# Gate and up products of 18 of 22 FFN tiles as seven block products for eight

## The chip, the cores and the metric

The kernel runs on one core of one Trainium2 chip. The metric is the device time of one execution, in microseconds (us). Of the kernel before, three runs took 2164.84 to 2165.06 us, median 2164.97.

## What is computed

Two layers of a streaming encoder trunk over 576 tokens: a sample stream of 64 and a prompt of 512. Each layer has three attention branches and then a gated feed-forward network (FFN), which is the part that the change touches:

```
xn = x * rsqrt(mean(x*x) + EPS) * g            # RMSNorm, D_MODEL 1024
gu = xn @ w_up                                 # 1024 x (2 * 2816): gate half, up half
c  = conv_b + sum over kk of conv_w[kk] * (gate with its two rows of state ahead)[t + kk]
x += (gelu(c) * up) @ w_down                   # 2816 x 1024
```

Inputs and outputs are float32.

## The kernel before

The tokens lie along the free dimension, features on the partitions, so the residual stream x is eight tiles `x1_00` to `x1_07` of 128x576. A TensorE product covers 288 tokens (a "half": the first has the 64 sample tokens and 224 of the prompt, the second 288 of the prompt). Every float32 product is made of two fp32r parts: each weight and each token tile is split into a high part (a cast by ScalarE) and a low part (source minus high, by VectorE), and three matmuls of 128x128 by 128x288 (hi·hi, hi·lo, lo·hi) are summed in PSUM (`mm`, L131 in the trace).

The 2816 columns of the FFN are 22 tiles f. Per tile there are two chunks: gate `g` (8 blocks of the 1024 rows x 2 halves x 3 = 48 matmuls into PSUM tiles `mg`) and up `u` (48, into `mu`). `ffn_f` (L1236) writes what follows them: VectorE multiplies the gate's product by the norm factor `R` into the convolution's input `gp`; ScalarE and VectorE make the convolution `c` (one activation, two scalar_tensor_tensor of 578 columns); ScalarE makes the gelu `ge`; VectorE makes `ur` = up x R; GpSimd multiplies `ge` by `ur`; ScalarE and VectorE split the result into `hh` and `hl`. The down product runs by groups of tiles, `FG = [2, 4, 4, 4, 4, 4]`: `down` (L1312) makes four chunks `d2` per group, each with two column blocks x two halves, every one of those four blocks a sum over the tiles of the group (3 matmuls per tile: 12 in a group of four, 6 in the group of two). Its PSUM tiles `md` come from a pool of two banks (`pmm`), and VectorE adds each block to x (`x<-md,x`). The four down chunks of a group follow one another after the first tile of the next group.

The order of the work is written by hand. `chunk` lists the chunks; `run_main` (L424) goes through them, emits the matmuls and, between them (`tick`), lets generators (`gens`) emit a step each, by a clock `clk` that adds up assumed costs per engine. `fetch` (L375, loads at L383) is called two chunks ahead and issues the load of a raw weight tile (128x8x128, 512 KB) on SyncE's queue; `split` (L385) makes its high and low parts one chunk ahead. So each engine runs a fixed list in order, and an instruction that waits holds what is behind it on its engine. All operations of ScalarE, VectorE and GpSimd go through one helper, and have the line L102 in the trace.

Of the kernel before, what the change touches and what calls it, by code (L numbers as in the profile page):

```python
# [16 lines left out]
P = 128  # L17
# [24 lines left out]
FG = [2, 4, 4, 4, 4, 4]  # L42


@with_exitstack
def trunk_kernel(ctx: ExitStack, tc: tile.TileContext, a: dict, o: dict):
# [16 lines left out]
    def slot(nm, dt=F32):  # L63
        return sp_.tile([P, TOK], dt, tag="s", name=nm, bufs=NS)

    def wide(tag, nm, dt=F32):
        return ap_.tile([P, 1280], dt, tag=tag, name=nm, bufs=2)
# [80 lines left out]
    def tick():  # L148
        now = clk["PE"]
        went = False  # L150
        for it in list(gens):
            if it[2] <= now and (it[0] == "w" or max(clk["ACT"], clk["DVE"]) < now + LAG):
                step(it)
                went = True
# [121 lines left out]
    def load_tables():  # L276
# [7 lines left out]
        t5t = sm.tile([32, 4], F32, tag="t5", name="t5t", bufs=1)  # L284
# [36 lines left out]
    def setup(aid, tabs, t5t, oh):  # L321
# [11 lines left out]
        for l in range(DEPTH):  # L333
# [5 lines left out]
            lt = sm.tile([P, 64], F32, tag="lt", name=f"lt{l}", bufs=1)  # L339
# [28 lines left out]
    def chunk(nm, src, kt, act, evac, ncol=1, pre=None, pre_ev=None, post=None, norm=None, half=None, twin=None):  # L368

        chunks.append(dict(nm=nm, src=src, kt=kt, act=act, evac=evac, ncol=ncol, pre=pre, pre_ev=pre_ev, post=post,  # L370
                           norm=norm, half=half))
# [3 lines left out]
    def fetch(i):  # L375
# [3 lines left out]
        if c["src"] is None:  # L379
            return  # L380
# [43 lines left out]
    def run_main(start):  # L424
        for i in range(start, len(chunks)):
# [3 lines left out]
            drain("w")  # L429
            fetch(i + 2)  # L430
            if i + 1 < len(chunks):
                spawn("w", split(i + 1), True)
            kt = c["kt"]
# [129 lines left out]
    def load_bias_sample(rows, nm):  # L563
        b = ap_.tile([P, 192], F32, tag="bias_s", name=f"biass{nm}", bufs=1)
# [5 lines left out]
    def natural(u, src, off, kind):  # L570
# [8 lines left out]
        nat = sm.tile([P, 4, P], F32, tag="nat", name=f"nat{kind}{nm}", bufs=1)  # L579
# [9 lines left out]
        else:  # L589
            nats = sm.tile([T, P], F32, tag="natsk", name=f"natsk{nm}", bufs=1)  # L590
# [8 lines left out]
    def prep_v(u):  # L599
# [6 lines left out]
        VS = ap_.tile([P, 4, 2, P], F32R, tag="VS", name=f"VS{nm}", bufs=2)  # L606
# [12 lines left out]
    def prep_k(u):  # L619
# [3 lines left out]
        KD = ap_.tile([P, 2, S], F32R, tag="KD", name=f"KD{nm}", bufs=1)  # L623
# [22 lines left out]
    def prep_q(u):  # L646
# [4 lines left out]
        X = ap_.tile([P, 2, S], F32R, tag="X", name=f"X{nm}", bufs=1)  # L651
# [133 lines left out]
    def sample_soft(u, nm, b):  # L785
# [6 lines left out]
        A = sm.tile([P, 256], F32, tag="sa", name=f"sA{nm}", bufs=1)  # L792
# [55 lines left out]
    def sample_b(u):  # L848
# [10 lines left out]
        A = sm.tile([P, 256], F32, tag="sa", name=f"sA{nm}", bufs=1)  # L859
# [11 lines left out]
    def head_b(u, e):  # L871
# [5 lines left out]
        ch = ap_.tile([P, 512], F32R, tag="bias", name=f"ch{nm}", bufs=2)[:, 0:384]  # L877
# [840 lines left out]
```

## Time and profile before

| | |
|---|---|
| median of 3 runs | 2164.97 us (2164.84 to 2165.06) |
| profiled execution, its own time | 2164.78 us |
| its span in the profile | 2163.0 us |
| mean granted TensorE clock | 0.999 of full |
| TensorE busy | 2135.8 us, 99% of the span, 15911 matmuls and transposes |
| VectorE, ScalarE, GpSimd busy | 64%, 48%, 18% |
| moved by DMA | 200.5 MB, mean 93 GB/s |

The FFN of layer 0 runs from about 659 to 1080 us, that of layer 1 from about 1722 to 2140 us. Matmuls are pipelined: the duration printed for one is longer than the distance to the next, so the rate is read from the distances of starts, or from a run of many in the chain of waits. A step on VectorE likewise can start a little ahead of the printed end of the one before.

### The profile page before, as it was taken

What the parts mean: (1) busy time and instruction counts of PE and PEld (TensorE: products, weight loads), DVE (VectorE), ACT (ScalarE), POOL (GpSimd) and SP (SyncE); (2) the same over time, 40 slices, a digit from 0 to 9 for tenths busy, and PEclk for the clock granted to TensorE, in tenths of its full rate; (3) what the DMA queues carried; (4) which work ended last, traced back from release to release, by engine and by line L of the source; (5) the groups of instructions that cost most, each with busy time, mean ns of one, the idle gap of its engine ahead of it and who ended that gap; (6) DMA issues with size and microseconds to landing.
All of it is one profiled execution on the core that took longest, in us unless ns stands there. A gap on an engine that the chain in (4) does not pass through costs nothing.

```text
span 2163.0 us, 39766 instructions
## 1 busy us (share of the span) xinstructions
PE 2135.8 (99%) x15911; PEld 2099.8 (97%) x15911; DVE 1393.0 (64%) x2860; ACT 1041.3 (48%) x2057; POOL 398.1 (18%) x523
## 2 busy tenths in 40 slices
PE   8999999999999999999999999999999999999998
PEld 7999999999999999999999999999999999999998
DVE  7886667767466655556678765667765566555564
ACT  5657776555434322323355677755554333222334
POOL 2111121111122111212110122201102112111221
PEclk9999999999999999999999999999999999999999
DMA  7442222223332322222243222233323322222222
GB/s 216 122 139 84 73 85 80 89 79 97 93 118 60 101 84 82 85 79 88 88 139 107 83 73 73 73 93 98 99 74 122 88 79 81 86 78 88 78 89 65
DMA packets 326563, 200.50 MB, mean 93 GB/s; under 512 B 10544, under 2 KB 320754, under 8 KB 326314
## 3 DMA queue, kind: packets, MB, share of 16 engines
q1 hardware_dynamic: 324618, 194.88, 30.6%
q0 software_dynamic: 1760, 3.08, 0.4%
q8 instruction: 125, 2.05, 0.4%
q14 instruction: 60, 0.49, 0.1%
HBM read 176.54 MB, written 25.83 MB: 94 GB/s over the span
## 4 chain that ended last, share of the span: by engine, by line
PE 92%; DVE 5%; issue 1%; ACT 1%; POOL 1%; DMA 0%; SPq 0%; DVEq 0%; POOLq 0%; ACTq 0%
PE md L131 11%; PE mg1f L131 6%; PE mg0f L131 6%; PE mu0f L131 6%; PE mu1f L131 6%; PE mo L131 4%; PE mg0a L131 2%; PE mg1a L131 2%; PE mg0b L131 2%; PE mg1b L131 2%; PE mg0c L131 2%; PE mg1c L131 2%; DVE wlod L102 1%; PE mb1a L131 1%; PE mb0a L131 1%
## 5 line engine op out<-in xcount | busy, mean ns | idle before, releaser
L102 DVE TENSOR_TENSOR x<-md,x 128x288 f32<-128x288 f32 x192 | 86.9, 455 | 117.2 <-PE md L131 116.3
L102 ACT CAST whid<-wrd 128x512 fp32r<-128x512 f32 (+1 forms) x88 | 46.8, 579 | 138.1 <-PE md L131 87.9
L131 PE MATMUL md<-hh0f,whid 128*128 128x288 f32 x352 | 104.9, 298 | 3.5 <-DVE x L102 3.5
L131 PE MATMUL mu0f<-xhf,wlou0f 128*128 128x288 f32 x352 | 103.8, 295 | 0.0
L131 PE MATMUL mu1f<-xhf,wlou1f 128*128 128x288 f32 x352 | 103.8, 295 | 0.0
L131 PE MATMUL md<-hh0f,wlod 128*128 128x288 f32 x352 | 103.8, 295 | 0.0
L131 PE MATMUL mg1f<-xhf,whig1f 128*128 128x288 f32 x352 | 103.7, 295 | 0.0
L131 PE MATMUL mg0f<-xhf,whig0f 128*128 128x288 f32 x352 | 103.7, 295 | 0.0
L131 PE MATMUL mg0f<-xhf,wlog0f 128*128 128x288 f32 x352 | 103.7, 295 | 0.0
L131 PE MATMUL mg1f<-xhf,wlog1f 128*128 128x288 f32 x352 | 103.7, 295 | 0.0
L131 PE MATMUL mu1f<-xlf,whiu1f 128*128 128x288 f32 x352 | 103.7, 295 | 0.0
L131 PE MATMUL mu0f<-xlf,whiu0f 128*128 128x288 f32 x352 | 103.7, 295 | 0.0
L131 PE MATMUL mu0f<-xhf,whiu0f 128*128 128x288 f32 x352 | 103.6, 294 | 0.0
L131 PE MATMUL mu1f<-xhf,whiu1f 128*128 128x288 f32 x352 | 103.6, 294 | 0.0
L131 PE MATMUL md<-hl0f,whid 128*128 128x288 f32 x352 | 103.6, 294 | 0.0
L131 PE MATMUL mg0f<-xlf,whig0f 128*128 128x288 f32 x352 | 103.6, 294 | 0.0
L131 PE MATMUL mg1f<-xlf,whig1f 128*128 128x288 f32 x352 | 103.6, 294 | 0.0
L131 PE MATMUL md<-hh1f,whid 128*128 128x288 f32 x288 | 85.7, 297 | 2.7 <-DVE x L102 2.7
L131 PE MATMUL md<-hh1f,wlod 128*128 128x288 f32 x288 | 84.9, 295 | 0.0
L131 PE MATMUL md<-hl1f,whid 128*128 128x288 f32 x288 | 84.8, 294 | 0.0
L131 PE MATMUL mo<-ml,whio 128*128 128x288 f32 x256 | 75.6, 295 | 0.8 <-DVE ml L102 0.8
L131 PE MATMUL mo<-mh,wloo 128*128 128x288 f32 x256 | 75.5, 295 | 0.0
(960 smaller groups left out, 8434.1 us busy)
## 6 DMA issues: line engine op xcount, KB each, us to landing
wrd<-in_w_down SPq DMA_DIRECT2D x40, 512.0 KB
wrg0f<-in_w_up SPq DMA_DIRECT2D x22, 512.0 KB
wru0f<-in_w_up SPq DMA_DIRECT2D x22, 512.0 KB
wrg1f<-in_w_up SPq DMA_DIRECT2D x22, 512.0 KB
wru1f<-in_w_up SPq DMA_DIRECT2D x22, 512.0 KB
wro<-in_w_out SPq DMA_DIRECT2D x16, 512.0 KB
xspill<-x SPq DMA_DIRECT2D x16, 288.0 KB
x<-xspill SPq DMA_DIRECT2D x16, 288.0 KB
```

The costliest lines, as they stand in the source:

```text
L102: return f(*args, **kw)
L131: nc.tensor.matmul(out, lhsT=lhsT, rhs=rhs, start=start, stop=stop, skip_group_check=True)
```

## The change

With the token halves h0 and h1, the rows of the weights cut into a top and a bottom half of 512, and gate and up as the two output blocks, gate and up of one tile are a product of 2x2 blocks: A11, A12 (gate, top and bottom rows), A21, A22 (up) times y11, y12 (top rows of y = x·g·R, halves h0, h1), y21, y22 (bottom rows). Eight block products of 12 matmuls each make 96. From tile NORD = 4 on, the change uses a seven-product scheme of Strassen's kind (84 matmuls), in the order A11, P, R, A12, Q, A22, V, with P = A21 + A22, R = A21 + A11, Q = P + A11, V = Q + A12.

- **Token side.** Once per layer, `forms` (L1320) makes y and its differences on VectorE in slots `ya`, `yb`, `tp`, `tq`, and their high and low parts `fh`, `fl` for seven forms, beside tiles 0 to 3. Some lows are a subtraction on VectorE, others (`low`, L1346) a copy of minus the high part by ScalarE and then an accumulating DMA of the source, issued on GpSimd's queue.
- **Weight side.** Per tile, `wforms` (L1386) loads A11|A12 (raw tile `wr..0`), A22 (`wr..3`) and A21 twice (`wr..1`), 1.25 MB for 1 MB. Two accumulating DMAs add A22 and A11 to the two copies of A21, which gives P and R. Two additions on VectorE give Q and V (`wr..2`). The high parts are casts by ScalarE; the lows of A11 and A12 (`wlo..a`) and of A22 (`el..d0`) are by ScalarE and accumulating DMA, those of P and R (`el..b0`, `el..b1`) and of Q and V (`wlo..c`) by VectorE.
- **Results.** `unit_f` (L1438) emits the 84 matmuls (A12 adds into the bank of A11, Q into that of P) and the combining: three kinds of copies by ScalarE (`s`, `gp`), five operations of VectorE (`z`, `u`, `s`, `u`, `gp`). No multiplication by R is left there, and the product ge·u moves from GpSimd to VectorE (`tail`, L1521).
- **Down product.** A down chunk follows each tile (two of them follow tiles 4 and 5, which belong to the first group of two tiles), with loads and splits of its own in slots (`down_own`, L1416: `dr` raw, `dh`, `dl`), where before four chunks ran in a row.
- **Memory.** The tiles of attention, FFN and end live in pools by phase; `gp`, `c`, `ge` move into slots.

```diff
...
 FG = [2, 4, 4, 4, 4, 4]
+NORD = 4
+GW = TOK + 4
...
+    phase = {"p": tc.alloc_tile_pool(name="att0", bufs=1, reuse_waits="tile")}
+    def next_phase(nm):
+        phase["p"].release()
+        phase["p"] = tc.alloc_tile_pool(name=nm, bufs=1, reuse_waits="tile")
+    def ptile(shape, dt, tag, name, bufs):
+        return phase["p"].tile(shape, dt, tag=tag, name=name, bufs=bufs)
     def wide(tag, nm, dt=F32):
-        return ap_.tile([P, 1280], dt, tag=tag, name=nm, bufs=2)
+        return ptile([P, 1280], dt, tag=tag, name=nm, bufs=2)
...
+            if c["own"] and c["src"] is None:
+                c["act"]()
+                continue
+            if c["own"]:
+                drain_while(lambda: not c.get("hi"), c["nm"])
...
+            chunk(f"u{nm}", a["w_up"][l][:, F + f * P:F + (f + 1) * P], ND, act, evu, pre_ev=pre_u, post=post_u,
+                  pre=(lambda: spawn("wf", wforms(NORD))) if f == NORD - 1 else None)
...
+        def forms():
+            R = cur["R"]
+            two = lambda t: t.rearrange("p (b c) -> p b c", b=2)
+            for k in range(4):
+                y1, y2, t12, t34 = (two(slot(f"{n}{l}{k}")) for n in ("ya", "yb", "tp", "tq"))
+                for y, d in ((y1, k), (y2, k + 4)):
+                    vector.scalar_tensor_tensor(y.rearrange("p b c -> p (b c)"), in0=x[d], scalar=gffn(l, d),
+                                                in1=R, op0=ALU.mult, op1=ALU.mult)
+                    yield
...
+                fh, fl = fast["fh"][k], fast["fl"][k]
+                for j, n, src in ((0, 1, y1[:, 0:1, :]), (1, 2, y2), (3, 2, t12), (5, 2, t34)):
+                    hi = fh[:, j:j + n, :]
+                    scalar.copy(hi, src)
+                    yield
+                    low(fl[:, j:j + n, :], src, hi, n == 2)
+                    yield
+        def low(out, src, hi, by_dma):
+            if by_dma:
+                scalar.activation(out, hi.bitcast(F32), AF.Copy, scale=-1.0)
+                charge("POOL", 900)
+                nc.gpsimd.dma_start(out, src, accum_op=ALU.add)
+            else:
+                vector.tensor_tensor(out, src, hi.bitcast(F32), op=ALU.subtract)
...
+        def wparts(f, nm, forms_, src, by_dma, small):
+            if f > NORD:
+                yield from until(lambda: all((f - 1, n) in used for n in forms_))
+            elif nm == "b":
+                yield from until(lambda: not any(g[0] == "forms" for g in gens))
+            elif nm in "cd":
+                yield from until(lambda: "go" in fast)
+            yield
...
+            for j, n in enumerate(forms_):
+                hi, lo = pairs[j]
+                scalar.copy(hi, src[:, 4 * j:4 * j + 4, :])
+                yield
+                low(lo, src[:, 4 * j:4 * j + 4, :], hi, by_dma)
+                ws[f, n] = (hi, lo)
+                made.add((f, n))
+                yield
+        def wforms(f):
+            if f >= NF:
+                return
+            if f > NORD:
+                yield from until(lambda: all((f - 1, n) in made for n, _ in SEQ))
...
+            a22 = half_tile(f"wr{l}{f}3")
+            dma(raw[0], rr(gc))
+            dma(a22, rr(uc[D // 2:D]))
+            for j in range(2):
+                dma(raw[1][:, 4 * j:4 * j + 4, :], rr(uc[0:D // 2]))
+            spawn("wa", wparts(f, "a", ("A11", "A12"), raw[0], True, False), True)
+            spawn("wd", wparts(f, "d", ("A22",), a22, True, True), True)
+            yield from pause(5000)
+            for j, t in enumerate((a22, raw[0][:, 0:4, :])):
+                charge("POOL", 900)
+                nc.gpsimd.dma_start(raw[1][:, 4 * j:4 * j + 4, :], t, accum_op=ALU.add)
+            yield from pause(5000)
+            spawn("wb", wparts(f, "b", ("P", "R"), raw[1], False, True), True)
+            q = raw[2]
+            vector.tensor_tensor(q[:, 0:4, :], raw[1][:, 0:4, :], raw[0][:, 0:4, :], op=ALU.add)
+            yield
+            vector.tensor_tensor(q[:, 4:8, :], q[:, 0:4, :], raw[0][:, 4:8, :], op=ALU.add)
+            yield
+            yield from wparts(f, "c", ("Q", "V"), q, False, False)
+        def down_own(c, fs, d2, after):
+            yield from until(after)
...
+            for j in range(2):
+                dma(raw[j], src[:, n * j:n * j + n, :])
+            yield from pause(4000)
+            hi, lo = ([slot(f"d{t}{key}{j}", F32R)[:, 0:n * 256].rearrange("p (k c) -> p k c", k=n)
+                       for j in range(2)] for t in "hl")
+            for j in range(2):
+                scalar.copy(hi[j], raw[j])
+                yield
+                vector.tensor_tensor(lo[j], raw[j], hi[j].bitcast(F32), op=ALU.subtract)
+                yield
...
+        SEQ = (("A11", 0), ("P", 3), ("R", 5), ("A12", 1), ("Q", 4), ("A22", 6), ("V", 2))
+        def unit_f(f):
...
+            b = {}
+            def done_(form):
+                ps = lambda i: b[i][0][1][:, 0:HALF]
+                if form == "A11":
+                    scalar.copy(s[:, h0], ps("A11"))
+                elif form == "P":
+                    scalar.copy(s[:, h1], ps("P"))
+                elif form == "A12":
+                    p_ = ps("A11")
+                    t0 = cx["t"]
+                    scalar.copy(gp[:, 68:292], p_[:, T:HALF])
+                    cx["t"] = t0
+                    scalar.copy(gp[:, 2:66], p_[:, 0:T])
+                    give(b["A11"])
+                elif form == "Q":
+                    vector.tensor_tensor(z, ps("P"), s[:, h0], op=ALU.add)
+                    give(b["P"])
+                    vector.tensor_tensor(u[:, h1], ps("R"), z, op=ALU.subtract)
+                    give(b["R"])
+                    vector.tensor_tensor(s[:, h1], s[:, h1], u[:, h1], op=ALU.add)
+                elif form == "A22":
+                    vector.tensor_tensor(u[:, h0], ps("A22"), s[:, h1], op=ALU.add)
+                    give(b["A22"])
+                elif form == "V":
+                    vector.tensor_tensor(gp[:, 292:580], ps("V"), z, op=ALU.add)
+                    give(b["V"])
+            for form, i in SEQ:
+                drain_while(lambda: (f, form) not in ws, form)
+                home = {"A12": "A11", "Q": "P"}.get(form, form)
+                if home == form:
+                    b[form] = now_bank("z", f"m{nm}{form}")
+                out = b[home][0][1][:, 0:HALF]
+                wh, wl = ws.pop((f, form))
+                for k in range(4):
+                    fh, fl = fast["fh"][k][:, i, :], fast["fl"][k][:, i, :]
...
+                    if k == 3:
+                        used.add((f, form))
+                        cx["t"] = clk["PE"] + 70
+                        done_(form)
+                    if form == "A11" and k == 0:
+                        spawn("wf", wforms(f + 1))
+                    tick()
+            spawn(f"f{l}{f}", tail(f, gp, u))
...
+        def tail(f, gp, u):
...
+            yield
+            vector.tensor_tensor(ge, ge, u, op=ALU.mult)
+            yield
+            h_, l_ = slot(f"hh{nm}", F32R), slot(f"hl{nm}", F32R)
+            scalar.copy(h_, ge)
+            yield
+            vector.tensor_tensor(l_, ge, h_.bitcast(F32), op=ALU.subtract)
+            hs[f] = (h_, l_)
...
+        owns, issued = [], set()
+        def all_own():
+            for n, (c, fs, d2) in enumerate(owns):
+                yield from down_own(c, fs, d2, lambda: n == 0 or n - 1 in issued)
+        downs = iter(())
         for gi, fs in enumerate(groups):
             for i, f in enumerate(fs):
-                ffn_f(f)
-                if gi and i == (len(fs) - 1 if gi == len(groups) - 1 else 0):
-                    down(groups[gi - 1], False)
+                if f < NORD:
+                    ffn_f(f)
+                    continue
+                chunk(f"x{l}{f}", None, 0, lambda f=f: (f == NORD and start_fast(), unit_f(f)), None, own=True)
+                for _ in range(2 if gi == 1 else 1):
+                    next(downs, None)
+            for _ in downs:
+                pass
+            downs = down(fs, False)
+            next(downs)
+        def start_fast():
+            drain("forms")
+            fast["go"] = True
+            spawn("wn", all_own())
```

The instructions that move, as the order of the programs shows them, at three places on VectorE.

First, a tile in the middle of layer 0 and the down block behind it. Before (from the end of the up product of tile 6 on; `wlod` are lows of down weights, `x1_0n<-md` the additions to x):

```order
L102 TENSOR_TENSOR ur0f6_9143<-mu0f601_9145,Rg0f0_8066 128x288
L102 TENSOR_TENSOR wlod021_9184<-wrd021_9104,whid021_9183 128x512 x2
L102 TENSOR_TENSOR x1_00_7479<-md02000_9176,x1_00_7479 128x288
L102 TENSOR_TENSOR hl0f6_9205<-ge0f6_9155,hh0f6_9204 128x576
L102 TENSOR_TENSOR x1_00_7479<-md02001_9197,x1_00_7479 128x288
L102 TENSOR_TENSOR x1_01_7481<-md02010_9215,x1_01_7481 128x288
L102 TENSOR_TENSOR x1_01_7481<-md02011_9229,x1_01_7481 128x288
L102 TENSOR_TENSOR wlod022_9250<-wrd022_9174,whid022_9249 128x512 x2
L102 TENSOR_TENSOR x1_02_7483<-md02100_9245,x1_02_7483 128x288
L102 TENSOR_TENSOR x1_02_7483<-md02101_9265,x1_02_7483 128x288
```

And with the change (tile 12, from its last product V on; `md06200` to `md06211` are the four blocks of its down chunk, `wr0132` the sums Q and V of tile 13, `el013b0`, `el013b1`, `wlo013c` its lows):

```order
L117 TENSOR_TENSOR gp0f12_10558<-m0f12V_10679,z0f4_8715 128x288
L117 TENSOR_TENSOR wr0132_10577<-wr0131_10576,wr0130_10575 128x512
L117 TENSOR_TENSOR x1_04_7490<-md06200_10701,x1_04_7490 128x288
L117 TENSOR_TENSOR wr0132_10577<-wr0132_10577,wr0130_10575 128x512
L117 TENSOR_TENSOR el013b0_10721<-wr0131_10576,eh013b0_10720 128x512
L117 SCALAR_TENSOR_TENSOR c0f12_10705<-gp0f12_10558,pcol01_1178,c0f12_10705 128x578 x2
L117 TENSOR_TENSOR x1_04_7490<-md06201_10726,x1_04_7490 128x288
L117 TENSOR_TENSOR wlo013c_10744<-wr0132_10577,whi013c_10743 128x512
L117 TENSOR_TENSOR el013b1_10723<-wr0131_10576,eh013b1_10722 128x512
L117 TENSOR_TENSOR x1_05_7492<-md06210_10746,x1_05_7492 128x288
L117 TENSOR_TENSOR ge0f12_10767<-ge0f12_10767,u0f12_10562 128x576
```

Between the first and the second addition to x there now stand a sum, a low and the two steps of the convolution.

Second, the two down chunks behind tile 4 (the first is `md000..`, the second begins with `md00100` and needs `dl0010` and `dl0011`; in the list before, the lows of a down chunk came one chunk ahead):

```order
L117 TENSOR_TENSOR x1_01_7484<-md00010_8889,x1_01_7484 128x288
L117 SCALAR_TENSOR_TENSOR c0f4_8873<-gp0f4_8711,pcol01_1178,c0f4_8873 128x578 x2
L117 TENSOR_TENSOR x1_01_7484<-md00011_8899,x1_01_7484 128x288
L117 TENSOR_TENSOR wr052_8777<-wr051_8776,wr050_8775 128x512
L117 TENSOR_TENSOR el05b0_8913<-wr051_8776,eh05b0_8912 128x512
L117 TENSOR_TENSOR ge0f4_8918<-ge0f4_8918,u0f4_8716 128x576
L117 TENSOR_TENSOR wr052_8777<-wr052_8777,wr050_8775 128x512
L117 TENSOR_TENSOR el05b1_8915<-wr051_8776,eh05b1_8914 128x512
L117 TENSOR_TENSOR hl0f4_8926<-ge0f4_8918,hh0f4_8925 128x576
L117 TENSOR_TENSOR dl0010_8930<-dr0010_8907,dh0010_8928 128x256
L117 TENSOR_TENSOR wlo05c_8934<-wr052_8777,whi05c_8933 128x512
L117 TENSOR_TENSOR dl0011_8931<-dr0011_8908,dh0011_8929 128x256
```

The lows of the second chunk stand behind the whole tail of tile 4 and the sums of tile 5.

Third, the way from tile 3 to tile 4, the first of seven products (`ur0f3` is the last of the old kind; `wr042` are the sums Q and V of tile 4; `ya03` to `fl03` the last forms of tokens; none of the last ten stood in the list before):

```order
L117 TENSOR_TENSOR ur0f3_8637<-mu0f301_8641,Rg0f0_8081 128x288
L117 TENSOR_TENSOR hl0f3_8682<-ge0f3_8653,hh0f3_8681 128x576
L117 TENSOR_TENSOR wr042_8612<-wr041_8611,wr040_8610 128x512
L117 TENSOR_TENSOR wr042_8612<-wr042_8612,wr040_8610 128x512
L117 SCALAR_TENSOR_TENSOR ya03_8690<-x1_03_7488,pcol00_1028,Rg0f0_8081 128x576
L117 SCALAR_TENSOR_TENSOR yb03_8691<-x1_07_7496,pcol00_1028,Rg0f0_8081 128x576
L117 TENSOR_TENSOR tp03_8692<-ya03_8690 128x288
L117 TENSOR_TENSOR tq03_8693<-ya03_8690,yb03_8691 128x288
L117 SCALAR_TENSOR_TENSOR tp03_8692<-tp03_8692,yb03_8691 128x288
L117 TENSOR_TENSOR tq03_8693<-tp03_8692,yb03_8691 128x288
L117 TENSOR_TENSOR fl03_8044<-ya03_8690,fh03_8040 128x288
L117 TENSOR_TENSOR el04b0_8729<-wr041_8611,eh04b0_8728 128x512
```

The two sums of weights, which wait for the accumulating DMAs into `wr041`, now stand ahead of the last token forms.

## Rows read from the trace of the kernel before

**Rows 1.** The page, part 1: busy us, share of the span, instructions.

```profile
PE 2135.8 (99%) x15911; PEld 2099.8 (97%) x15911; DVE 1393.0 (64%) x2860; ACT 1041.3 (48%) x2057; POOL 398.1 (18%) x523
```

**Rows 2.** Windows, FFN of layer 0: length, PE, PEld, DVE, ACT, POOL, clock, DMA share, GB/s.

```profile
659.20:1080.00 420.80, 417.47 (x3127) 414.76 (x3125) 249.53 (x416) 136.23 (x240) 79.00 (x112) 1.00 0.28 84
```

**Rows 3.** Chain that ended last, layer 0: start, length, what.

```profile
666.91 6.36 PE mu0f L131 x48
...
768.21 6.89 PE md L131 x50
```

**Rows 4.** Waits of TensorE, whole span: us in total, times, longest.

```profile
PE md L131 <- DVE x L102: 6.2, 15, 0.7
```

**Rows 5.** Timeline, TensorE: start, duration, what, [idle before, releaser].

```profile
719.98 0.29 PE L131 MATMUL mu0f<-xhf,whiu0f 128*128 128x288 f32 x1
...
767.55 0.29 PE L131 MATMUL md<-hh0f,wlod 128*128 128x288 f32 x1
768.21 0.40 PE L131 MATMUL md<-hh0f,whid 128*128 128x288 f32 x1 [0.37 <-DVE x L102]
768.45 0.29 PE L131 MATMUL md<-hl0f,whid 128*128 128x288 f32 x1
```

**Rows 6.** Timeline, VectorE, around three places of layer 0.

```profile
720.18 0.46 DVE L102 TENSOR_TENSOR gp0f<-mg0f,Rg0f 128x288 f32<-128x288 f32 x1 [2.67 <-PE mg0f L131]
...
746.14 1.30 DVE L102 TENSOR_TENSOR wlog0f<-wrg0f,whig0f 128x512 fp32r<-128x512 f32 x2
747.44 1.68 DVE L102 SCALAR_TENSOR_TENSOR c0f<-gp0f,pcol,c0f 128x578 f32<-128x578 f32 x2
...
767.71 0.45 DVE L102 TENSOR_TENSOR x<-md,x 128x288 f32<-128x288 f32 x1
768.08 0.75 DVE L102 TENSOR_TENSOR hl0f<-ge0f,hh0f 128x576 fp32r<-128x576 f32 x1
```

**Rows 7.** VectorE by line and form, 700 to 1080: busy, mean ns, idle before.

```profile
L102 DVE TENSOR_TENSOR wlou0f<-wru0f,whiu0f 128x512 fp32r<-128x512 f32 x38 | 43.1, 1175 | 1.8
...
L102 DVE TENSOR_TENSOR wlog0f<-wrg0f,whig0f 128x512 fp32r<-128x512 f32 x38 | 24.6, 689 | 1.1
L102 DVE TENSOR_TENSOR wlod<-wrd,whid 128x256 fp32r<-128x256 f32 x6 | 3.0, 543 | 0.0
```

**Rows 8.** GpSimd by line and form, same stretch.

```profile
L102 POOL TENSOR_TENSOR ge0f<-ge0f,ur0f 128x576 f32<-128x576 f32 x20 | 37.7, 1883 | 115.0 <-ACT whiu0f L102 86.0 <-ACT whid L102 29.1
```

**Rows 9.** Timeline, ScalarE, tile of layer 0.

```profile
745.49 1.14 ACT L102 CAST whig0f<-wrg0f 128x512 fp32r<-128x512 f32 x2 [2.98 <-PE mg0f L131]
```

**Rows 10.** DMA issues of GpSimd's queue: count, KB each, median us to landing.

```profile
ewin<-ebias POOLq DMA_DIRECT2D x1, 768.0 KB, 11.6
...
out_sa_k<-in_cache_a_k POOLq DMA_DIRECT2D x2, 128.0 KB, 3.2
out_sa_v<-in_cache_a_v POOLq DMA_DIRECT2D x2, 128.0 KB, 4.4
```

**Rows 11.** Timeline, GpSimd and SyncE: one DMA issue on each queue.

```profile
158.23 0.51 POOL L363 DMA_DIRECT2D out_sa_k<-in_cache_a_k  x1
...
734.74 0.37 SPq L383 DMA_DIRECT2D wru0f<-in_w_up  x1
```

**Rows 12.** Windows of half a us behind that load of 512 KB.

```profile
737.00:737.50 0.50, 0.50 (x6) 0.50 (x5) 0.00 (x0) 0.20 (x1) 0.00 (x0) 1.00 1.14 346
...
738.00:738.50 0.50, 0.50 (x6) 0.50 (x5) 0.00 (x0) 0.00 (x0) 0.00 (x0) 1.00 0.03 10
```

**Rows 13.** Windows of half a us at the end, behind the last matmul.

```profile
2155.50:2156.00 0.50, 0.10 (x1) 0.00 (x0) 0.18 (x2) 0.25 (x1) 0.00 (x0) 1.00 0.00 0
...
2157.50:2158.00 0.50, 0.00 (x0) 0.00 (x0) 0.50 (x2) 0.50 (x2) 0.00 (x0) 0.59 0.07 29
2158.00:2158.50 0.50, 0.00 (x0) 0.00 (x0) 0.50 (x1) 0.20 (x1) 0.00 (x0) 0.50 1.02 385
```

More of the change, by code (lines that the diff above doesn't have):

```diff
@@ L378, in fetch @@
         c = chunks[i]
-        if c["src"] is None:
+        if c["src"] is None or c["own"] or "raw" in c:
             return
@@ L429, in run_main @@
             drain("w")
+            if c["own"] and not all(n["own"] for n in chunks[i + 1:i + 3]):
+                drain("wa", "wb", "wd", "wf")
             fetch(i + 2)
-            if i + 1 < len(chunks):
+            if i + 1 < len(chunks) and not chunks[i + 1]["own"]:
                 spawn("w", split(i + 1), True)
+            if c["own"] and c["src"] is None:
[3 more added lines that the diff above has]
+                drain_while(lambda: not c.get("hi"), c["nm"])
             kt = c["kt"]
@@ L1074, in unit @@
         roomy = 4 * br + p < ROOMY
-        row = lambda n: slot(n) if roomy else ap_.tile([P, TOK], F32, tag="qv", name=n, bufs=1)
+        row = lambda n: slot(n) if roomy else ptile([P, TOK], F32, "qv", n, 1)
         def pre_v():
@@ new lines, in wforms @@
+        def wforms(f):
[3 more added lines that the diff above has]
+                yield from until(lambda: all((f - 1, n) in made for n, _ in SEQ))
+            w = a["w_up"][l]
+            gc, uc = w[:, f * P:(f + 1) * P], w[:, F + f * P:F + (f + 1) * P]
+            rr = lambda t: t.rearrange("(k p) c -> p k c", p=P)
+            raw = [wp.tile([P, 8, P], F32, tag="raw", name=f"wr{l}{f}{i}", bufs=3) for i in range(3)]
+            a22 = half_tile(f"wr{l}{f}3")
[17 more added lines that the diff above has]
+            yield from wparts(f, "c", ("Q", "V"), q, False, False)
@@ L1320, in ev @@
                 return go
+            if last:
+                for d2 in range(4):
+                    chunk(f"d{l}{fs[0]}{d2}", down_w(fs, d2), len(fs),
+                          lambda: ([hs[f][0] for f in fs], [hs[f][1] for f in fs]), ev(d2), ncol=2,
+                          pre=down_pre(fs, d2, last))
+                return
             for d2 in range(4):
+                yield
                 chunk(f"d{l}{fs[0]}{d2}", down_w(fs, d2), len(fs),
                       lambda: ([hs[f][0] for f in fs], [hs[f][1] for f in fs]), ev(d2), ncol=2,
-                      pre=down_pre(fs, d2, last))
+                      pre=down_pre(fs, d2, last), post=lambda n=len(owns): issued.add(n), own=True)
+                owns.append((chunks[-1], fs, d2))
         def down_final(fs):
@@ L1388, in final_begin @@
     def final_begin():
[L1389 removed]
+        cur["acc"] = ofw("facc")
         cur["xg"] = []
@@ L1656, in trunk_kernel @@
     final()
+    phase["p"].release()
 _INS = ['x_prompt', 'x_sample', 'cache_a_k', 'cache_a_v', 'cache_b_k', 'cache_b_v', 'cache_c_k', 'cache_c_v',
```

148 lines of the change are left out of this document (101 added, 47 removed).

## The prediction

> **What bounds the kernel now.** I read the page's busy table first: TensorE is busy for 2135.8 us of the span, VectorE for 1393.0 [rows 1]. The windows of the FFN say the same of the stretch that is changed: TensorE works in 417.47 of 420.80 us, VectorE in 249.53, ScalarE in 136.23, at full clock [rows 2]. The chain of waits gives the price of a matmul: 48 of them take 6.36 us, 0.1325 us each [rows 3]. So the time falls by what leaves TensorE, as long as the others keep up; and what they must newly do is read from the order, in which each engine holds everything behind an instruction that waits. The sum below is made against the profiled execution, 2164.8 us, which is 0.2 us from the median.
>
> **Removed.** Twelve matmuls for each of 36 tiles (18 in each of two layers): 432 x 0.1325 = **−57.2 us**. TensorE's order outside the FFN stays as it is. The waits of `md` for VectorE, 6.2 us in 15 places [rows 4], belong mostly to the old runs of down chunks: **−5**.
>
> **How the prices on VectorE are read.** An addition to x starts 0.37 us before the next instruction (767.71 to 768.08) though its duration is 0.45 [rows 6]: in a full queue an instruction takes its printed duration less about 0.09. So 128x288 takes 0.37, 128x576 0.66, two of 128x512 1.30 and so 0.65 each, the convolution's two steps 1.60 [rows 6], 128x256 0.45 (0.543 printed) [rows 7]. The result of a block is read 0.20 us after the next block has begun (719.98, 720.18) [rows 5, 6], and TensorE starts 0.05 after VectorE's end (767.71 + 0.45, 768.21) [rows 5, 6]. A restart costs 0.11: the next matmul follows after 0.24 and not 0.13 (768.21, 768.45) [rows 5].
>
> **A tile in the middle, on the path.** With the change one down chunk follows the last product V, four blocks of 12 matmuls, 1.59 us each, in two banks. The fourth block needs the bank of the second, which the second addition to x frees. By the order, VectorE has between the first and the second addition: a sum of weights, a low, and the convolution. From V's end: first block 1.59, its addition begins at +0.20 and holds 0.37; sum 0.65, low 0.65, convolution 1.60, second addition 0.45, release 0.05: 5.56 us. The fourth block could start at 3 x 1.59 = 4.77. Late by 0.79, with the restart 0.90. Sixteen tiles (6 to 21) in two layers: 32 x 0.90 = **+28.8 us**. Bounds: nothing, if these instructions run 21% faster than in these rows; and with 1175 ns for the low, the price of a low beside GpSimd's work [rows 7], 1.4 per tile, 45 in all. I take the middle, since GpSimd's product leaves this stretch.
>
> **The rest of a middle tile, at no cost.** TensorE needs 84 + 48 matmuls, 17.5 us. By the order and these prices VectorE has 12.7 us of work in it and ScalarE about 11.1, which TensorE covers. The raw weights: a load of 512 KB issued at 734.74 moves its last bytes before 738.0 [rows 11, 12], at most 3.3 us, and 1.8 MB in 17.5 us is 105 GB/s, where one slice carried 346 [rows 12]. The copy that the sums go into is refilled from half a us before the tile; its load has landed some 3.2 us into the tile, both accumulating DMAs are issued 0.5 us later [rows 11], and VectorE comes to the first sum at 11.7 us, behind its step for V. So up to 8 us of landing cost nothing. The nearest rows for a DMA of GpSimd's queue are 3.2 and 4.4 us for 128 KB, and, far off, 11.6 for 768 KB to memory [rows 10]. I take 4.4, the row nearest in size (256 KB). SyncE's next loads stand behind the same refill and are wanted a tile later. The memory pools by phase move nothing in TensorE's order; their hand-over waits for readers long done.
>
> **Entry into tile 4, on the path.** Here nothing runs ahead. Counted from the end of tile 3's up product: VectorE has `ur` at 0.65; GpSimd's product takes 1.88 [rows 8] and stands ahead of the DMA into the sums, so that one is issued at 2.55 and lands at 7.0. Only then VectorE passes the two sums (1.30), and the last `ya` and `yb` behind them (1.6): 9.9. ScalarE has eleven instructions of 0.57 to 0.63 and one of 0.35 from there to the high part of R, 6.9 us (a cast of 128x512 is 0.57 [rows 9]): 16.8. The low of R 0.65 and a hand-over: 17.6. Ten matmuls of R still follow, 1.3, so R ends at 19.0, where 36 matmuls would have ended at 4.77. Late by 14.3, twice: **+28.6 us**. With a landing of 3.2 it is 13.1 each; with 11.6, and a second landing (the token lows) in the same chain, up to 23.
>
> By the Trainium skill, "DMA: Bandwidth & Descriptors", section "Anatomy of one DMA — SWDGE (gpsimd) path", such a DMA takes 2.0 us and the bytes at 436 GB/s, 2.6 us for 256 KB (an estimate). The rows' 3.2 and 4.4 for half the bytes [rows 10] speak against so little. By the page both entries would be 1.8 us shorter and the sum 2195; I go by the rows.
>
> **The second down chunk of tiles 4 and 5, on the path.** Its weights are split in the slots behind the first one's. In VectorE's order `dl0011` stands behind three additions to x, the convolution, the fourth addition, two sums, two lows, the product, `hl0f4` and another two lows; counted with the prices above it is done 10.45 us after V. The last matmul of the first block that needs it would have come at 3.84: late by 6.6, with restarts 6.9. For tile 5 the same count gives 6.4. Two layers: 2 x 13.3 = **+26.6 us**. The bound below is half, if ScalarE and VectorE find part of it done; above, 1.5 each if lows cost 1175 ns [rows 7].
>
> **The clock.** Each of these six pauses (an entry and two chunks per layer) leaves TensorE idle for several us. At the end of the trace the last matmul begins a half us that shows 0.10 of work, at 2155.5; the granted clock is 1.00 up to 2157.5, 0.59 in the next half us, then 0.50, which is 1.2 GHz [rows 13]. There it fell some two us after the last matmul; twelve matmuls at that level would cost another 1.59. How soon it comes back no row shows. I take 2 us per pause, between 0 and 4: **+12 us**.
>
> **The sum.** 2164.8 − 57.2 − 5 + 28.8 + 28.6 + 26.6 + 12 = 2198.6, say **2199 us**. Its own bounds: landings of 3.2 and no clock loss, 2184; the clock at 4 each and a late landing at the entries, 2225.
>
> **Rivals.**
>
> *A, faster: VectorE's queue is quick enough in the middle tiles.* The place is the second addition to x; the price is the 28.8, and with the same speed some 10 of the second chunks and 4 of the entries: 2199 − 43 = 2156 us. It decides where what VectorE does from the first addition to the release takes under 3.0 us and not 3.8. For it: GpSimd's elementwise work, beside which a low takes 1175 and not 689 ns [rows 7], is gone from these tiles. Against it: I have taken the lower prices already, and the step order is fixed. 0.15.
>
> *B, much slower: accumulating DMAs land late in every tile.* At 11.6 us [rows 10], 3.6 over the 8 that are free, some 30 tiles give 108 and the entries 14: 2320 us; at 9.6, 48 and 10: 2257. For it: five such DMAs per tile, each read and write, on one queue; and VectorE and GpSimd do hinder each other here, 1175 against 689 ns [rows 7]. Against it: 3.2 and 4.4 us at 158 us into the span, where they were issued within 2 us of each other. 0.12. The longest unbroken piece of VectorE's list in a tile is 3.3 us (addition, sum, low, convolution); a DMA held for all of it would land after 7.7, still inside the 8.
>
> The Trainium skill, "SBUF — State Buffer", section "SBUF: two separate sides", has a rule that speaks for B: while VectorE holds the port pair that it shares with GpSimd, GpSimd cannot write the descriptors of its DMAs. The lows' 1175 ns agree that the two share something; no run here shows a DMA held.
>
> *C, slower: the clock stays down through the next unit.* If TensorE stays at 1.2 GHz for some 8 us after each of six pauses, that is 48 instead of 12: 2235 us. Rows show the fall [rows 13], none the return. 0.06.
>
> *D, no change: the pauses at tiles 4 and 5 are half as long*, since instructions of ScalarE that I put behind the sums are done before them: −27.6, and half the clock: −6, so 2165 us. For it: the planner emits by its own clock, and the entry's count rests on twelve instructions in a row. 0.07.
>
> That the change does not do what it says is excluded: the order shows the twelve matmuls gone from each of 36 tiles.
>
> **How the numbers follow.** The forecast has 0.60 (2184 to 2225), A 0.15 (about 2156), B 0.12, C 0.06 (2235), D 0.07 (2165). A range of 2152 to 2240 holds all but B and the edges of the rest. Within 0.2%, 4.3 us, which is about what a measurement of this kernel can tell, lie D and a little of A: 0.09. Faster by more: the rest of A, 0.14. Slower: 0.77.
>
> **What would show it.** In the profile of the changed kernel: TensorE's busy time falls by some 57 us while its idle time rises to about 110; in the middle tiles a wait of `md` for `x` of 0.8 us once per tile; in each layer one pause of about 14 us in R of tile 4 and two of over 6 in the second down chunks, with granted clocks under 1.00 behind them, and full clock elsewhere; accumulating DMAs that land within 5 us. Wrong would be: no idle time of `md` in tiles 6 to 21 (A), waits of VectorE's sums for a DMA in every tile (B), or long stretches at 0.50 (C).

## The result and the profile after the change

The changed kernel takes 2186.86 us (median of four runs, 2185.4 to 2188.15) against 2164.98: a ratio of 1.0101, 95% interval 1.0083 to 1.0118. It is slower by 1.0%, with 432 matmuls fewer. The prediction was 2199 us, 2152 to 2240. The execution profiled below took 2187.04 us by its own time.

The page of the profile after, busy us and share of the span (2185.2 us) by engine [rows 1]:

```profile
PE 2105.9 (96%) x15479; PEld 2059.1 (94%) x15479; DVE 1447.1 (66%) x3024; ACT 1226.4 (56%) x2473; POOL 471.6 (22%) x691
```

Windows after: the FFN of layer 0 [rows 2], then in it the entry into tile 4 up to the end of product R, the two down chunks behind tile 4, and a middle tile (length, PE, PEld, DVE, ACT, POOL, clock, DMA share, GB/s):

```profile
658.70:1091.00 432.30, 402.35 (x2914) 394.29 (x2913) 277.55 (x498) 228.17 (x449) 115.88 (x196) 0.96 0.70 156
710.96:731.72 20.76, 9.44 (x38) 7.72 (x37) 9.43 (x17) 11.92 (x23) 9.46 (x12) 0.59 1.08 201
738.09:752.50 14.41, 9.48 (x50) 8.71 (x49) 10.74 (x20) 5.11 (x10) 2.23 (x6) 0.76 0.86 185
788.30:806.57 18.27, 17.73 (x134) 17.50 (x133) 11.74 (x21) 9.84 (x20) 4.59 (x10) 1.00 0.78 173
```

A middle tile has 132 matmuls, 17.49 us at 0.1325, and takes 18.25 to 18.34. The entry has 36, 4.77 us, and takes 20.76. The two chunks have 48, 6.36 us, and take 14.41. TensorE's waits after, largest first, from the start of the list of waits [rows 4]:

```profile
PE md L146 <- DVE x L117: 17.8, 35, 0.5
PE md L146 <- ACT dh L117: 15.9, 4, 4.6
PE m1f4A L146 <- ACT fh L117: 6.0, 1, 6.0
PE m0f4A L146 <- ACT fh L117: 5.8, 1, 5.8
PE md L146 <- DVE dl L117: 2.8, 4, 1.1
```

Each of the places that the prediction named has its row: the second addition to x in the middle tiles (32 of the 35 times; the other three stand in the last down chunks of layer 0), the second down chunks (`dh`, four times), the entry (`m0f4A`, `m1f4A`). The middle tile on the timeline, TensorE and then VectorE [rows 5, 6]:

```profile
793.76 0.40 PE L146 MATMUL md<-hh0f,dh 128*128 128x288 f32 x1 [0.54 <-DVE x L117]
```

```profile
790.09 0.46 DVE L117 TENSOR_TENSOR x<-md,x 128x288 f32<-128x288 f32 x1 [0.51 <-PE md L146]
790.46 0.68 DVE L117 TENSOR_TENSOR wr<-wr,wr 128x512 f32<-128x512 f32 x1
791.06 0.69 DVE L117 TENSOR_TENSOR el07b<-wr,eh07b 128x512 fp32r<-128x512 f32 x1
791.66 1.68 DVE L117 SCALAR_TENSOR_TENSOR c0f<-gp0f,pcol,c0f 128x578 f32<-128x578 f32 x2
793.25 0.45 DVE L117 TENSOR_TENSOR x<-md,x 128x288 f32<-128x288 f32 x1
```

V ends at 788.30. Sum, low and convolution lie between the two additions, and the fourth down block starts at 793.76, 5.46 us behind V; the working had 5.56. The entry, VectorE and then TensorE:

```profile
717.20 1.42 DVE L117 TENSOR_TENSOR wr<-wr,wr 128x512 f32<-128x512 f32 x2 [2.11 <-DMA wr<-wr]
718.54 0.81 DVE L117 SCALAR_TENSOR_TENSOR ya<-x,pcol,Rg0f 128x576 f32<-128x576 f32 x1
```

```profile
719.87 0.61 PE L146 MATMUL m0f4A<-fh,whi04a 128*128 128x288 f32 x1 [5.77 <-ACT fh L117]
722.10 0.61 PE L146 MATMUL m0f4A<-fl,whi04a 128*128 128x288 f32 x1 [1.63 <-DVE fl L117]
...
724.62 0.61 PE L146 MATMUL m0f4P<-fh,eh04b 128*128 128x288 f32 x1 [1.67 <-ACT eh04b L117]
...
728.36 0.61 PE L146 MATMUL m0f4P<-fl,eh04b 128*128 128x288 f32 x1 [0.73 <-DMA fl<-tp]
```

The up product of tile 3 ends at 710.96, and the sums start 6.2 us later (7.0 in the working), held by the accumulating DMA; behind them stand the last token forms, and A11 needs their high part.

### The profile page after: what moved, and what is told of

It reads as the page before. It is cut to its first block, busy times and chain, and to the rows that moved or that the text cites. A ratio compares the mean times of both kernels' runs of the same rounds, so it can differ in the third digit from the quotient of the medians.

```text
span 2185.2 us, 40161 instructions
## 1 busy us (share of the span) xinstructions
PE 2105.9 (96%) x15479; PEld 2059.1 (94%) x15479; DVE 1447.1 (66%) x3024; ACT 1226.4 (56%) x2473; POOL 471.6 (22%) x691
## 4 chain that ended last, share of the span: by engine, by line
PE 89%; DVE 6%; issue 2%; DMA 1%; ACT 1%; POOL 1%; SPq 0%; DVEq 0%; POOLq 0%; ACTq 0%
PE md L146 12%; PE mo L146 4%; PE mg1a L146 2%; PE mg0a L146 2%; PE mg1b L146 2%; PE mg0b L146 2%; PE mg1c L146 2%; PE mg0c L146 2%; DVE x L117 1%; PE mb1a L146 1%; PE mb0a L146 1%; PE mv1b L146 1%; PE mv0b L146 1%; PE mv1a L146 1%; PE mv1c L146 1%
## 5 line engine op out<-in xcount | busy, mean ns | idle before, releaser
L1406 POOL DMA_DIRECT2D wr<-wr x72 | 64.2, 976 | 320.3 <-DMA wr<-in_w_up 254.0
L146 PE MATMUL md<-hh1f,dh 128*128 128x288 f32 x288 | 89.2, 310 | 16.4 <-DVE x L117 8.5
L146 PE MATMUL md<-hh0f,dh 128*128 128x288 f32 x288 | 88.9, 309 | 16.4 <-DVE x L117 8.5
L146 PE MATMUL md<-hh1f,dl 128*128 128x288 f32 x288 | 87.4, 303 | 1.4 <-DVE dl L117 1.4
L146 PE MATMUL md<-hh0f,dl 128*128 128x288 f32 x288 | 87.2, 303 | 1.4 <-DVE dl L117 1.4
L146 PE MATMUL md<-hl1f,dh 128*128 128x288 f32 x288 | 86.7, 301 | 0.0
L146 PE MATMUL md<-hl0f,dh 128*128 128x288 f32 x288 | 86.7, 301 | 0.0
L146 PE MATMUL mo<-mh,whio 128*128 128x288 f32 x256 | 75.8, 296 | 0.0
L146 PEld LDWEIGHTS md<-hh1f,dh 128*128 128x128 f32 x288 | 56.1, 195 | 20.8 <-DVE x L117 12.2
L146 PEld LDWEIGHTS md<-hl1f,dh 128*128 128x128 f32 x288 | 56.1, 195 | 0.0
```

Source lines behind the costliest of these rows:

```text
L146: nc.tensor.matmul(out, lhsT=lhsT, rhs=rhs, start=start, stop=stop, skip_group_check=True)
L1406: nc.gpsimd.dma_start(raw[1][:, 4 * j:4 * j + 4, :], t, accum_op=ALU.add)
```

## The experiments

Every time below is a median of runs beside the kernel before, which took 2164.8 us in them. "Less" and "more" are against the kernel after the change (2187). "Over" is the time of a stretch less 0.1325 us for each of its matmuls, worked out from their starts.

**Convolution behind the second addition.** All tiles of seven products; nothing else is edited.

```diff
...
-            yield
+            yield from pause(late) if late else iter((None,))
             vector.scalar_tensor_tensor(c[:, 2:580], in0=gp[:, 1:579], scalar=convw(l, 1, f), in1=c[:, 2:580],
...
-            ge = yield from conv_steps(f, gp)
+            ge = yield from conv_steps(f, gp, 3300)
```

> Edit: in the tiles of seven products the two VectorE steps of the convolution are emitted 3.3 us later, behind the second addition of the down block to x. Theory (the convolution holds the second addition, and so the bank of the fourth down block): each of 32 middle tiles loses the 0.80 us that it takes over its 132 matmuls, 32 x 0.80 = 26 us, so about 2161 us; the pauses at tiles 4 and 5 stay. Rival 1 (the convolution's delay is paid elsewhere: the gelu on ScalarE waits for it and holds the casts of the next tile's weights): the 0.8 moves to the products P or R, and the time stays within 8 us of 2187. Rival 2 (it is the additions themselves that are late): no change, 2187.

2170.94 us (2169.22 to 2171.74), 16 less. Its waits of `md` for `x` show the cause, the list of waits of the whole run:

```profile
PE md L146 <- ACT dh L117: 19.1, 4, 4.9
...
PE md L146 <- DVE x L117: 2.3, 5, 0.8
```

35 waits have become 5, none of them in tiles 6 to 20. These tiles run at 0.00 over where they had 0.80: 30 x 0.80 = 24 us. Some 8 came back: in layer 0 the two chunks behind tile 4 grew from 8.05 to 9.03 over, and the last run of down chunks, which needs tile 21's product at once, from 2.5 (with tile 21's own 0.8) to 4.3. So the mechanism is shown, and the expected 2161 us was missed by what a later convolution makes late behind it.

**Second down chunk split earlier.**

```diff
-                yield from down_own(c, fs, d2, lambda: n == 0 or n - 1 in issued)
+                yield from down_own(c, fs, d2, lambda: n == 0 or n - 1 in issued or (n == 1))
```

> Edit: the second down chunk (behind tile 4) is loaded and split at once, not only when the first has been emitted; the fourth (behind tile 5) as before. Theory (the pause is the place of the split in the lists, behind the tail of tile 4): the first pause of each layer, 8.05 us with its lower clock, falls to under 1.5, and the one of tile 5, 7.1 us, stays: 2 x 6.5 to 2 x 8 less, 2171 to 2174 us. Rival (ScalarE and VectorE have no room for it earlier, since the entry into tile 4 is full): the entry grows by what the pause loses, 2187.

2179.93 us (2179.02 to 2182.36), 7 less. In layer 0, TensorE's list of waits from 735 to 775 has one wait for `dh` where there were two, the one behind tile 5:

```profile
PE md L146 <- ACT dh L117: 4.7, 1, 4.7
```

Behind tile 4 the over falls from 8.05 to 1.71, with the granted clock at 1.00; behind tile 5 it rises from 7.14 to 8.73. The place in the lists sets the pause, as the theory says, and a quarter of the gain moved on to the next one, so that the time stayed above the 2171 to 2174 us that were expected. The rival is out: the entry did not grow by what the pause lost.

**Sums of tile 4 behind the token forms.**

```diff
+            if f == NORD:
+                yield from until(lambda: not any(g[0] == "forms" for g in gens))
             q = raw[2]
```

> Edit: the two sums of weights of tile 4 stand behind the last token forms in VectorE's list, and not ahead of them. Theory (the sums wait for the accumulating DMA until 717.20 and hold the forms, for which the first product waits 5.77 and 1.63 us): the forms start at 715.0, behind hl0f3, 3.5 us earlier, and the entry is 3.5 to 5 us shorter in each layer: 2177 to 2180 us. Rival 1 (the landing itself sets the end): P waits for its sum as long as before, no more than 1 us per layer is won, 2185 or more. Rival 2 (GpSimd's queue of accumulating DMAs for the token lows sets it): the same, with the waits for fl.

2191.79 us (2190.91 to 2192.44), 5 more: a miss. The waits of the entry in this run, the list of waits from 710 to 733:

```profile
PE m0f4P L146 <- DMA fl<-tp: 3.8, 1, 3.8
PE m0f4A L146 <- ACT fh L117: 2.0, 1, 2.0
```

A11's wait for `fh` went from 5.8 to 2.0, as expected, and P's wait for a token low from 0.7 to 3.8. The DMA issues of this run from 713 to 726 show why (KB each, us to landing):

```profile
...
fl<-tp POOLq DMA_DIRECT2D x2, 288.0 KB, 7.1
fl<-tq POOLq DMA_DIRECT2D x2, 288.0 KB, 7.6
wr<-wr POOLq DMA_DIRECT2D x2, 256.0 KB, 4.4
...
```

In the kernel after, the same two rows of token lows, from 713 to 728, have 5.6 and 6.3. With the forms earlier, their DMAs are issued from 718.5 to 721.1, while those of the token lows before them, issued at 714.6 and 716.1, are still under way (until 720.6 and 722.3). The one that P waits for takes 8.3 us, where it took 5.25. Rival 2 held: at the entry the head of VectorE's queue was only the first of several bounds. The entry stayed as long as it was (16.24 over in layer 0). In layer 0 the chunks behind tiles 4 and 5 grew besides, from 8.05 and 7.14 to 9.34 and 8.17 over, and that made the total worse than before the edit.

**A filler to keep the clock.** Thirty useless matmuls ahead of the first block of the second and fourth down chunk.

```diff
...
+                    if j == 0 and h == 0 and c["nm"][2:] in ("01", "03") and c["own"]:
+                        for _ in range(30):
+                            nc.tensor.matmul(pp, lhsT=tri[:, 0:P], rhs=warm["fh"], start=True, stop=False, skip_group_check=True)
...
```

> Edit: the kernel after the change, with 30 matmuls of no use (about 4.0 us) ahead of the first block of the second and of the fourth down chunk, into the bank that this block overwrites; they lie inside the pause of 4.9 us there. Theory (part of each pause is the clock, which is 0.50 for 6.8 us behind it): the clock stays at 1.00 at four places, and each unit becomes 1.5 to 2.5 us shorter: 4 to 10 us less, 2177 to 2183 us. Rival (behind the pause VectorE sets the pace, whatever the clock): no change, 2187, or some 3 us more if the filler runs beyond the wait.

2187.04 us (2186.12 to 2188.14): nothing won. Its windows, during the filler, the first matmuls behind it, and then:

```profile
741.00:745.00 4.00, 4.00 (x31) 3.85 (x30) 3.96 (x7) 1.63 (x4) 0.00 (x0) 1.00 0.94 167
746.00:748.00 2.00, 1.06 (x6) 0.60 (x5) 2.00 (x5) 0.99 (x3) 0.00 (x0) 1.00 0.66 186
748.20:751.30 3.10, 3.10 (x15) 3.10 (x14) 1.18 (x4) 0.00 (x0) 0.00 (x0) 0.50 1.00 276
```

The clock holds during the filler and while the six matmuls behind it wait for the lows `dl`; then it falls all the same, for 3.4 us and not 6.8. The part that it gives back is the part in which VectorE's lows set the pace, and behind tile 5 the filler runs past the wait (14.36 us for the chunks, not 13.50). So this run doesn't separate the price of the clock; it stays a reading of rows: in the kernel after, the 19 matmuls from 748.17 on take until 752.50, 4.3 us and not 2.5, about 1.8 us in such a pause.

**The entry alone.** The core of the edit:

```diff
-                  post=lambda: (spawn(f"c{l}{f}", conv()), spawn("forms", forms()) if f == 0 else None))
+                  post=lambda: (spawn(f"c{l}{f}", conv()), [spawn("forms", forms(ks)) for ks in ((0, 2), (1, 3))] if f == 0 else None))
...
-                    low(fl[:, j:j + n, :], src, hi, n == 2)
+                    low(fl[:, j:j + n, :], src, hi, n == 2 and k < 3)
...
-                low(lo, src[:, 4 * j:4 * j + 4, :], hi, by_dma)
+                low(lo, src[:, 4 * j:4 * j + 4, :], hi, by_dma and f > NORD)
```

> Edit, at the entry alone: the token forms are made by two generators side by side and not one, the last token lows by VectorE and not by DMA, the loads and sums of tile 4 begin one chunk earlier, the lows of tile 4's A11, A12, A22 and the product of tile 3 are done by VectorE and not on GpSimd's queue. Theory (in the run with the sums behind the forms, P waited 3.8 us for a token low whose DMA took some 7 us to land among the other DMAs there, so work and DMAs that crowd at the entry set it, and VectorE idles beside it): the entry falls from 16.0 us to 1 to 4 in each layer, the clock stays up: 24 to 30 us less, 2157 to 2163 us, if the pauses at tiles 4 and 5 stay. Rival (another wait takes the place, as the token lows did): 2180 or more.

2166.7 us (2165.64 to 2167.68), 20 less, where 24 to 30 were expected. One wait is left at the entry of layer 0, from 700 to 722:

```profile
PE m0f4P L146 <- DVE el04b L117: 1.1, 1, 1.1
```

The entry is 1.8 us over in layer 0 and 1.1 in layer 1, from 16.0 and 16.2. So the entries gave 29 us. Some 4 of them went to the tiles ahead, where an up product waits 1.7 us per layer for a token low on ScalarE, and 4 to the chunks behind tile 4 (9.69 over in layer 0, where they had 8.05). The run changes several things at once: it shows that the entry can be freed, and not which of them freed it.

**All edits together.** The entry's, the convolution 2.0 us later in tiles 4 to 20, and

```diff
-                yield from down_own(c, fs, d2, lambda: n == 0 or n - 1 in issued)
+                yield from down_own(c, fs, d2, lambda: n < 2 or n - (2 if n < 4 else 1) in issued)
```

> Edit: the edits of the entry, the convolution 2.0 us later in tiles 4 to 20, and the down chunks of tiles 4 and 5 split one chunk earlier, together. Theory (the four terms are separate waits, and the clock falls only behind pauses): entry −26, the two pauses of each layer from 8.05 and 7.1 to under 2 each, −24, middle tiles −20: 2187 − 70, about 2117 us, 2112 to 2126; the granted clock is 1.00 throughout the FFN. Rival (with TensorE at its full pace the weights of the next tile come late: P and R wait some 0.7 us per tile for their lows): 32 x 0.7 more, about 2140.

2118.32 us (2117.63 to 2119.07), a ratio of 0.9785 to the kernel before (0.9771 to 0.980): faster by 2.1%, and by 3.1% than the change as it was made. Its page, and the FFN of layer 0 in its windows:

```profile
PE 2083.2 (98%) x15479; PEld 2045.8 (97%) x15479; DVE 1456.0 (69%) x3038; ACT 1217.9 (58%) x2461; POOL 489.0 (23%) x677
```

```profile
658.00:1065.00 407.00, 398.91 (x2975) 395.38 (x2974) 286.93 (x514) 228.94 (x450) 128.06 (x191) 1.00 0.72 164
```

These are the same matmuls and sums as in the change, in another order, with some lows of the entry and the product of tile 3 moved to VectorE. The two chunks behind tiles 4 and 5 are 2.2 and 1.2 us over, the middle tiles 0.0. Two new waits appear, in the list of waits of the whole run: one for a low of P in tile 7 of layer 0 (0.6 us in layer 1), and one in an up product of layer 1:

```profile
PE m0f7P L146 <- DVE el07b L117: 1.8, 1, 1.8
PE mu1f L146 <- DVE gp1f L117: 1.8, 1, 1.8
```

The granted clock is 1.00 in the FFN of layer 0. In layer 1 it fell once, which was not expected: behind the second of these waits it is 0.50 from 1722.4 to 1725.6.

**Sums P and R by VectorE instead of accumulating DMAs.**

```diff
-                charge("POOL", 900)
-                nc.gpsimd.dma_start(raw[1][:, 4 * j:4 * j + 4, :], t, accum_op=ALU.add)
+                vector.tensor_tensor(raw[1][:, 4 * j:4 * j + 4, :], raw[1][:, 4 * j:4 * j + 4, :], t, op=ALU.add)
+                yield
```

> Edit: the kernel after the change, with the sums P and R of the weights made by VectorE (two additions of 128x512, 1.3 us per tile) and not by accumulating DMAs; the lows by DMA stay. Theory (in the middle tiles the landing of these DMAs is hidden, and VectorE has room: 12.7 + 1.3 of 18.3 us): middle tiles as they are, the entry 2 to 4 us shorter in each layer, since the sums no longer wait for a DMA: 2179 to 2187 us. Rival (the additional steps stand between the first and the second addition to x, or hold the casts of P and R): 0.65 to 1.3 more in each of 32 tiles, 2205 to 2225.

2195.01 us (2194.55 to 2196.75), 8 more. Between theory and rival: from tile 10 on the middle tiles lose the 0.80 at `md` and are 0.87 over in P instead. TensorE in tile 11 of this run:

```profile
874.05 0.40 PE L146 MATMUL m0f11P<-fh,el011b 128*128 128x288 f32 x1 [0.61 <-DVE el011b L117]
```

VectorE had time for 1.3 us more, but not in every place of its list: the two additions push the low of P back. This exchange costs next to nothing. Most of the 8 us lies in tile 9, which is 5.3 us over in each layer (tiles 6 to 8 are 0.2 or less), with waits in P and R and a granted clock of 0.90 (830.25 to 846.69). The list of waits of the whole run has them:

```profile
PE m0f9R L146 <- ACT eh09b L117: 1.5, 1, 1.5
...
PE m0f9P L146 <- DVE el09b L117: 1.2, 1, 1.2
```

Why it is this tile was not followed further. The entry became only 0.6 and 1.0 us shorter.

## Why the prediction was right, and where its numbers were off

The direction, the range and the three kinds of places were right; within the entry the wait lay elsewhere, and the time was 12 us too long. By terms, in us:

| term | predicted | in the trace after |
|---|---|---|
| 432 matmuls removed | −57.2 | −57.2 |
| waits of the old down runs | −5 | −9.8 |
| middle tiles, 32 | +28.8 | 32 x 0.80 = +25.6 |
| entry, two, with its share of the clock | +28.6 + 4 | +32.2 |
| second down chunks, four, with theirs | +26.6 + 8 | +30.8 |
| sum on 2164.8 | 2198.6 | 2186.4 (measured 2187.0) |

- **Removed.** The rate of a matmul stayed. The old waits were mis-sized: the 6.2 us of [rows 4] are the idle times alone. Counted as time over 0.1325 per matmul, the down runs that went had 4.9 us in each layer: each wait brings its restart, and in the first run of each layer, 2.35 us over, the additions to x stood behind lows of weights in VectorE's list.
- **Middle tiles.** The mechanism is shown by the run with the later convolution; the size was 0.80 and not 0.90. From the first addition to the release VectorE took 3.67 us and not 3.77, since the sum and the low held it for 0.60 each (790.46, 791.06, 791.66), where the working had 0.65. Its own rule, the printed 0.69 less 0.09, gives 0.60.
- **The rest of a middle tile at no cost** held. VectorE is busy for 11.74 us of it, ScalarE for 9.84 (12.7 and 11.1 in the working). The accumulating DMAs into the sums landed after 4.4 us in the median, the value taken, and after 7.5 at most, inside the 8 that were free, and VectorE waited for them at the two entries only, as the row of the sums shows (72 sums, idle before them 4.4 us in all):

```profile
L117 DVE TENSOR_TENSOR wr<-wr,wr 128x512 f32<-128x512 f32 x72 | 49.4, 686 | 4.4 <-DMA wr<-wr 4.3
```

That decides against rival B. One premise was wrong without consequence: the tile moves 173 GB/s and not 105, at 0.78 of the DMA engines' time, because the five accumulating DMAs move 1.3 MB that I had not counted.
- **Entry.** The chain was right up to the sums (6.2 us, with 7.0 in the working). The step that failed is where the wait lies: I put it in R, for the low of its weights; it lay mostly in A11, for the high and low parts of the last token form, 7.4 of the 11.3 us that TensorE idled there in layer 0. The total, 16.0 over where I had 14.3 and 2 for the clock, agrees in part by luck: the idle time was 3 us less, and the other 4.7 us are restarts and matmuls at a granted clock of 0.50, 0.24 us apart and not 0.1325:

```profile
725.99 0.44 PE L146 MATMUL m0f4P<-fl,eh04b 128*128 128x288 f32 x1
726.23 0.44 PE L146 MATMUL m0f4P<-fh,el04b 128*128 128x288 f32 x1
```

The landing of the token lows, which the prediction had in its upper bound alone, is a second bound close behind, as the run with the sums behind the forms showed.
- **Second down chunks.** The list on VectorE was right: `dl0011` was wanted by a matmul that began 10.1 us behind V (748.17, V ending at 738.09), where the working had 10.45. What the working did not have is that TensorE idled first and longest for the high part `dh`, 15.9 us in the four chunks and 2.8 for the lows. On ScalarE it stands behind `hh`, which waits for VectorE's product, in the same tail of tile 4:

```profile
745.01 0.67 ACT L117 CAST hh0f<-ge0f 128x576 fp32r<-128x576 f32 x1 [0.95 <-DVE ge0f L117]
745.59 0.40 ACT L117 CAST dh<-dr 128x256 fp32r<-128x256 f32 x1
```

With the clock the four chunks have 30.8 us over, where 34.6 were forecast.
- **The clock** fell in all six pauses, as forecast. Behind the first down chunk of tile 4 it was 0.50 for 6 us of work, then full, in windows of the kernel after:

```profile
746.00:752.00 6.00, 5.61 (x21) 5.07 (x22) 3.94 (x9) 1.34 (x3) 0.00 (x0) 0.50 0.83 218
752.10:755.00 2.90, 2.90 (x24) 2.90 (x23) 0.52 (x2) 0.40 (x1) 1.37 (x2) 1.00 0.35 96
```

Through the first 2 us of it the matmuls would have waited for the lows anyway; the rest is the 1.8 us worked out under the filler, where I had taken 2 and rival C 8. At the entry it is more, about 4 of the 4.7 us named there (an estimate: five restarts at 0.11 taken off). The price rests on these distances: the filler did not show it by itself.
- **Rival A** fell with the waits of `md` for `x` in all 32 middle tiles (3.67 us, where it needed less than 3.0); **D** with the full length of the pauses.
- **One of the signs did not come.** TensorE's busy time fell by 29.9 us (2135.8 to 2105.9) and not by 57, and its idle time is 79 us and not 110. Busy time goes by printed durations, which grow behind each wait and at half the clock: 9.44 us in the entry for 4.77 of matmuls, 9.48 in the two chunks for 6.36, 17.73 in a middle tile for 17.49.

By the Trainium skill, "DMA: Bandwidth & Descriptors", section "Anatomy of one DMA — SWDGE (gpsimd) path", a DMA of 256 KB on GpSimd's queue takes 2.6 us (an estimate from its fit). The trace has 4.4 as the median of the 72 accumulating ones, and the measurement decides.

## What to carry to other kernels

Fewer matmuls pay only where every other engine's list has room at the right place: here 67 us were saved (57 of them in matmuls) and 89 lost, with VectorE busy for two thirds of the time and the DMAs of the middle tiles landed in time. What costs is what stands ahead in the queue: put the step that frees a PSUM bank ahead of long elementwise work, prepare the first unit of a new kind as far ahead as the later ones, and issue a DMA so early that it has landed when the queue comes to the step that needs it; moving that step back alone made this kernel 5 us slower. And undo such waits together: three of the edits alone gave part of their gain to the next wait, and all of them gave 68.5 us.

## What the runs showed of the hardware

- An accumulating DMA's issue (256 KB) holds GpSimd for about 1 us, where a plain one of 128 KB had taken 0.51 [rows 11]. The row of the kernel after, by line: busy us, mean ns of one:

```profile
L1406 POOL DMA_DIRECT2D wr<-wr x72 | 64.2, 976 | 320.3 <-DMA wr<-in_w_up 254.0
```

- They land after 4.4 us in the median (72 of 256 KB in the kernel after, 3.3 to 7.5). The token lows of 288 KB that met at the entry in the run with the sums behind the forms took 6.0 to 8.9.
- The 1175 ns of a low beside GpSimd's work [rows 7] is a mean of two sizes. Of the 38 lows, 23 took 0.69 us: 8 with no product of GpSimd's beside them, and 15 that began 0.07 us ahead of one. The other 15 began 0.54 us behind the start of such a product, and took 1.92.
- The granted clock fell at different distances from the last matmul: two us at the program's end [rows 13], four behind the first down chunk of tile 4 (last matmul at 741.17, still 1.00 in a window up to 745.0), and under one at the entry, where a run of seven matmuls between two waits had begun its last at 713.80. Windows of the kernel after:

```profile
741.50:745.00 3.50, 0.00 (x0) 0.00 (x0) 3.46 (x7) 1.28 (x3) 0.00 (x0) 1.00 1.02 184
745.30:746.00 0.70, 0.00 (x0) 0.00 (x0) 0.70 (x2) 0.70 (x3) 0.00 (x0) 0.50 0.00 0
713.00:714.30 1.30, 1.10 (x7) 0.86 (x7) 0.00 (x0) 0.67 (x2) 1.30 (x3) 1.00 1.03 183
714.60:719.80 5.20, 0.00 (x0) 0.00 (x0) 3.06 (x5) 1.38 (x3) 2.49 (x3) 0.50 1.04 176
```

- A filler in a pause moved the fall of the granted clock to a time 3 us behind the filler's end, when TensorE was at work again; it did not avoid it.
